# Two decoder layers on one core: a chunk's outputs issued with the next chunk's work, a merge in halves, and a longer pause in front of the scores

## The chip, the core and the metric

The kernel runs on one core of one Trainium2 chip. The core has five engines with an instruction queue each: TensorE (PE, matrix products, with its weight loads shown apart as PEld), VectorE (DVE), ScalarE (ACT), GpSimd (POOL) and SyncE (SP, which here only issues DMAs). They run on their own and wait for each other through semaphores. The metric is the time of one execution on the device in microseconds (us), lower is better: the median of three runs before is 1919.49 us (1916.85 to 1920.4). In rows of the trace, L117 and L133 are lines of two helpers that issue every matmul and every VectorE or ScalarE operation, so an operation is known by its tiles, written out<-in.

## What is computed

Two layers of a decoder, 256 tokens, width 2048, all in float32. The first joins an RG-LRU and an mLSTM group; the change doesn't touch it. The second is RWKV-7 time mixing with 64 heads of 64: an input projection gives r, k, v and a gate z, low-rank paths give the decay w and the rate a, and each head carries a 64x64 state S from token to token:

```python
def step(S, inp):
    r_t, w_t, k_t, v_t, kk_t, a_t = inp
    sa = jnp.einsum('bhvk,bhk->bhv', S, -kk_t)
    S = (S * w_t[:, :, None, :] + sa[..., None] * (kk_t * a_t)[:, :, None, :]
         + v_t[..., None] * k_t[:, :, None, :])
    return S, jnp.einsum('bhvk,bhk->bhv', S, r_t)
...
kk = (k * k_k).astype(jnp.float32).reshape(B, S, H, d)
kk = kk / jnp.maximum(jnp.sqrt(jnp.sum(kk * kk, axis=-1, keepdims=True)), 1e-12)
...
y = rwkv7_scan(rh, wh, kh, vh, kk, ah)
y = head_norm(y.reshape(B, S, RWKV_WIDTH), H, RWKV_GN_EPS, gn_g, gn_b)
bonus = jnp.sum(rh * kh * r_k.astype(jnp.float32), axis=-1, keepdims=True) * vh
y = (y + bonus.reshape(B, S, RWKV_WIDTH)).astype(h.dtype)
return (y * jax.nn.silu(z)) @ w_out
```

The kernel takes the 256 tokens in four chunks of 64. Inside a chunk the dependence of the tokens on each other becomes a triangular system of 64x64 for each head, which is inverted once; from chunk to chunk the state is carried.

## The kernel before

**Projections.** The second layer works in eight groups g of eight heads (four tiles f of 128 features, two heads hd in each). A group has four projections in the order k, r, z, v (`in_proj`, line 242), each of eight pieces. A piece loads 512 KB of weights, splits them in a rounded part whi (ScalarE, CAST) and the rest wlo (VectorE) in `split_w` (line 202), and multiplies: hh·whi and hl·whi in turn, then hh·wlo, 24 matmuls of 128x256 a piece (`in_mms`, line 221) into banks called `gb`. hh and hl are the two parts of the normed input. whi and wlo have three buffers each. The splits are emitted at a higher priority than other work, so that the scheduler puts them ahead of it on ScalarE and VectorE.

**Weaving.** The rest of a group is written as Python generators in five lanes of `Weave` (line 58). After every four projection matmuls `tick(0.44)` moves a planner's clock on, and generators whose time has come are advanced; what they issue stands at that place in PE's order, which `InOrder` makes fixed. A `yield w` asks for w planner's microseconds before the next piece; after a piece with matmuls other generators are held back for 0.4. So a larger number in a yield moves the matmuls behind it later among the projection's, and whatever is later in the same lane with it. Lane 0 has `blocks` and `inverse`, lane 1 `scores`, `values` and `recur`, lane 2 the first half of `norm`, lane 3 `decay` and `keys`, lane 4 `outs`. Small matmuls write banks called `mb`, of which there are four.

**The pieces.** `keys` (line 851) works on the shifted k (kt, from `shifted`, line 806: a ScalarE copy and a VectorE operation for each of four tiles): squares sq on ScalarE, eight matmuls `cs,sq` for the norms, Gn from them, the product kP, and then eight times xx and zz (ScalarE, three buffers in common) and BK = xx·zz (VectorE); AR holds kk times the decay. `blocks` (line 891) multiplies BK by AR, 32 matmuls of 64x64 in four quarters, and VectorE makes Aab from them. `inverse` (line 950) eliminates on VectorE in blocks of 32 and merges them: 32 matmuls `ZT,Aab`, two copies to ZT on ScalarE, 32 matmuls `TT,ZT`, two copies to TT. `scores` (line 915) writes r times the decay into the other half of AR (four VectorE operations, line 919), pauses (`yield 2`, line 921), and makes At and the transposed BKt from AR and BK, tile by tile. `recur` (line 1043) then goes through the chunks c: W from UV and At; Ws, a copy; U from Ws and TT; UV, U times Gn on VectorE; S from UV and BKt; the new state Sn on VectorE, copied into the next chunk's UV by ScalarE; the outputs from UV and At; and, from c = 1 on, the outputs of the state before, from Rc and that state. W, U, S and each kind of output are eight matmuls. After c = 1 `norm` of the first 128 tokens is added in lane 2; that of the rest is done in `outs`.

**Groups overlap.** The recurrence of group g runs while the k projection and the r projection of group g+1 are on PE, so it meets `keys` and `blocks` of group g+1, on PE as on VectorE and ScalarE.

Of the kernel before, what the change touches and what calls it, by code (L numbers as in the profile page):

```python
# [7 lines left out]
F32 = mybir.dt.float32  # L8
# [3 lines left out]
ADD, SUB, MUL, MAX, MIN = ALU.add, ALU.subtract, ALU.mult, ALU.max, ALU.min  # L12

P = 128
# [130 lines left out]
def two_layers(ctx, tc, x, gpost, cst, selc, v0, v1, w_in0, w_out0, w_in1, w_out1, lruw, qkvw,  # L145
               wif, gbias, lora1, lora2, out):
    nc = tc.nc
    act, dve, pool, pe = nc.scalar, nc.vector, nc.gpsimd, nc.tensor
    PS = bass.MemoryType.PSUM
    wv_ = Weave(tc, 5)  # L150
    pe = wv_.pe = InOrder(tc, pe)
    dve, act = Behind(tc, dve), Behind(tc, act)
# [13 lines left out]
    def mbank():  # L166
        return pm.tile([P, 512], F32, name="mb", tag="mb")
# [252 lines left out]
    with ExitStack() as l0:  # L420
# [4 lines left out]
        def t4(name):  # L425
            return tp.tile([P, 4, T], F32, name=name, tag="t4")
# [315 lines left out]
    with ExitStack() as l1:  # L742
        c1 = l1.enter_context(tc.tile_pool(name="c1", bufs=1))
        g1 = l1.enter_context(tc.tile_pool(name="g1", bufs=1))
# [170 lines left out]
        def scores(g, st):  # L915
            rt, AR, BK, Pe = st["r"], st["AR"], st["BK"], st["Pe"]
            yield 0.36
            for f in range(4):
                dve.tensor_tensor(AR[:, f, :, 64:128], c4(rt[:, f, :]), Pe[:, 4 * f:4 * f + 4, 1:65], MUL)
                yield 0.5  # L920
            yield 2
            Rc = gt("Rc", "Rc", (4, 4, 64))
            act.copy(Rc, AR[:, :, :, 64:128])

            At = gt("At", "At", (4, 2, 4, 128))
            BKt = gt("BKt", "BKt", (4, 4, 128))
            rm4 = rmask.unsqueeze(1).broadcast_to([P, 4, 128])
            for f in range(4):
                ab = [mbank(), mbank()]
                for c in range(4):  # L930
                    for hd in range(2):
                        hr = slice(64 * hd, 64 * hd + 64)
                        pe.matmul(ab[hd][:, 128 * c:128 * c + 128], lhsT=BK[hr, f, c, :], rhs=AR[hr, f, c, :],
                                  start=(c == 0), stop=True, skip_group_check=True)
                b = mbank()
                for c in range(4):
                    pe.transpose(out=b[:, c * P:(c + 1) * P], in_=BK[:, f, c, :], identity=ident)
                yield 0.42
                for hd in range(2):
                    v = ab[hd].rearrange("p (c j) -> p c j", c=4)  # L940
                    dve.tensor_tensor(At[:, f, hd, :, :], v, rm4, MUL)
                    yield 1.12
                act.copy(BKt[:, f, :, :], b.rearrange("p (c j) -> p c j", c=4))
            for hd in range(2):
                hr = slice(64 * hd, 64 * hd + 64)
                act.copy(At[hr, :, hd, :, 0:64], AR[hr, :, :, 0:64])
                yield 0.3
            st.update(At=At, BKt=BKt, Rc=Rc)

        def inverse(g, st):  # L950
            Aab = st["Aab"]

            Ab, Tb, ZT = (t4(n, (32, 32), parts=64) for n in ("Ab", "Tb", "ZT"))
# [17 lines left out]
            TT = gt("TT", "TT", (32, 64))  # L971
# [8 lines left out]
            Amm = Aab.rearrange("p f h c i -> p (f h c) i")  # L980
            halves = [slice(16 * hf, 16 * hf + 16) for hf in range(2)]
            zb = [mbank(), mbank()]
            for m in range(32):
                pe.matmul(zb[m // 16][32:64, 32 * (m % 16):32 * (m % 16) + 32], lhsT=Amm[0:32, m, 32:64], rhs=ZT[0:32, m, :],
                          start=(m % 16 == 0), stop=True, skip_group_check=True)
            for hf, ms in enumerate(halves):
                act.copy(ZT[32:64, ms, :], zb[hf][32:64, :].rearrange("p (m c) -> p m c", m=16))
            yield 2.4
            tb = [mbank(), mbank()]
            for m in range(32):  # L990
                pe.matmul(tb[m // 16][0:32, 32 * (m % 16):32 * (m % 16) + 32], lhsT=ZT[32:64, m, :], rhs=TT[32:64, m, 32:64],
                          start=(m % 16 == 0), stop=True, skip_group_check=True)
            for hf, ms in enumerate(halves):
                act.copy(TT[0:32, ms, 32:64], tb[hf][0:32, :].rearrange("p (m c) -> p m c", m=16))
            yield 1.28

            TTv = TT.rearrange("p (f h c) i -> p f h c i", f=4, h=2)
            act.copy(TTv[64:128, :, 0, :, :].rearrange("p f c i -> p f (c i)"), TTv[0:64, :, 1, :, :].rearrange("p f c i -> p f (c i)"))
# [44 lines left out]
        def recur(g, st):  # L1043
            yield from until(st["inv"])
            At, BKt, UV, Rc, Gn, PC, TTv = (st[n] for n in ("At", "BKt", "UV", "Rc", "Gn", "PC", "T"))

            vt = st["v"]
            Yn = gt("Yn", "Yn", (2, 4, 2, 64))
            Yb = None
            St = None  # L1050
            for c in range(4):
                wb = mbank()
                for f in range(4):
                    for hd in range(2):
# [18 lines left out]
                Sp = St  # L1073
                if c < 3:
                    sb = mbank()
                    for f in range(4):
                        for hd in range(2):
                            hr = slice(64 * hd, 64 * hd + 64)
                            pe.matmul(sb[hr, f * 64:(f + 1) * 64], lhsT=BKt[:, f, c, hr], rhs=UV[:, c, f, hd, :],
                                      start=(f == 0), stop=True, skip_group_check=True)  # L1080
                    Sn = g1.tile([P, 4, 64], F32, name="Sn", tag="Sn", bufs=2)
                    sv = sb[:, 0:256].rearrange("p (f v) -> p f v", f=4)
                    pcb = PC[:, :, c:c + 1].broadcast_to([P, 4, 64])
                    if c:
                        dve.tensor_tensor(Sn, St, sv, ADD)
                        dve.tensor_tensor(Sn, Sn, pcb, MUL)
                    else:
                        dve.tensor_tensor(Sn, sv, pcb, MUL)
                    for hd in range(2):
                        hr = slice(64 * hd, 64 * hd + 64)  # L1090
                        act.copy(UV[hr, c + 1, :, hd, :], Sn[hr])
                    St = Sn
                    yield 2.4

                if c % 2 == 0:
                    Yb = [mbank(), mbank()]
                cr = [slice(64 * ((c + hd) % 2), 64 * ((c + hd) % 2) + 64) for hd in range(2)]
                for f in range(4):
                    for hd in range(2):
                        pe.matmul(Yb[hd][cr[hd], f * 64:(f + 1) * 64], lhsT=At[:, f, hd, c, 64:128],  # L1100
                                  rhs=UV[:, c, f, hd, :], start=(f == 0),
                                  stop=(c == 0), skip_group_check=True)
                yield 0.2
                if c:
                    for f in range(4):
                        for hd in range(2):
                            hr = slice(64 * hd, 64 * hd + 64)
                            pe.matmul(Yb[hd][cr[hd], f * 64:(f + 1) * 64], lhsT=Rc[hr, f, c, :],
                                      rhs=Sp[hr, f, :], start=False, stop=True, skip_group_check=True)
# [199 lines left out]
```

## Time and profile before

| | us |
|---|---|
| runs before, median (lowest, highest) | 1919.49 (1916.85, 1920.4) |
| the profiled execution | 1918.59 |
| its span in the profile | 1916.8 |
| PE busy | 1889.9 |
| DVE busy | 1395.0 |
| ACT busy | 1045.3 |
| mean granted clock of PE | 0.994 of full speed |

The span is the profiled execution from its first to its last instruction. Busy times are those in which at least one instruction of an engine was running; matmuls overlap in PE's pipeline, so starts tell more of their pace than durations. A row of the waits reads: engine and output waited on, the operation that released it, us in total, how often, the longest. A row of the timeline reads: start, duration, engine, operation with its tiles and shapes, how many were put together, and in brackets the idle time just before and what ended it. A row of the windows has its stretch, its length, the busy time and count of PE, PEld, DVE, ACT and POOL, then the granted clock, the share of DMA and GB/s. A row of the groups has busy time and mean ns behind the first bar, and the engine's idle time just before and what ended it behind the second.

### The profile page before, as it was taken

To read this page: it belongs to the slowest core of one execution; us is meant where nothing else is said; L and a number is where in the kernel's file an instruction comes from. 1 tells how busy PE (TensorE), PEld (TensorE's weight loads), DVE (VectorE), ACT (ScalarE), POOL (GpSimd) and SP (SyncE) were. 2 spreads that over 40 slices of the span, in tenths; PEclk is the share of its full clock that TensorE was granted. 3 is DMA by queue.
4 is the path that set the end of the run, shared out by engine and by line. 5 is a ranking of instruction groups with operands and counts; after the bars stand their busy time and mean duration, and the time that the engine had idled before them with its cause. 6 is when DMAs were issued, how large, how long until landed. Compare 5 with 4: busy or idle time off the path is not lost.

```text
span 1916.8 us, 39532 instructions
## 1 busy us (share of the span) xinstructions
PE 1889.9 (99%) x16507; PEld 1752.9 (91%) x16507; DVE 1395.0 (73%) x2302; ACT 1045.3 (55%) x1609; POOL 58.4 (3%) x84
## 2 busy tenths in 40 slices
PE   9999999999999999999999999999999999999998
PEld 8999999999888899989999999999999999997886
DVE  5667777767555579879689689597696896895544
ACT  6445666645444546555565555655655655555442
POOL 0000000000000000000000000000000000000000
PEclk9999999999999999999999999999999999999999
DMA  7333445445655444433343334344343343355664
GB/s 255 138 132 111 176 165 171 154 171 199 212 203 204 161 148 143 155 106 137 133 140 133 133 130 157 109 147 143 114 154 133 130 144 133 122 184 191 224 202 156
DMA packets 86947, 299.63 MB, mean 156 GB/s; under 512 B 9576, under 2 KB 12392, under 8 KB 86768
## 3 DMA queue, kind: packets, MB, share of 16 engines
q1 hardware_dynamic: 86768, 297.11, 45.0%
q8 instruction: 129, 2.11, 0.4%
q14 instruction: 50, 0.41, 0.1%
HBM read 289.20 MB, written 7.86 MB: 155 GB/s over the span
## 4 chain that ended last, share of the span: by engine, by line
PE 92%; DVE 5%; ACT 1%; issue 1%; DMA 1%; POOL 0%; SPq 0%; DVEq 0%; POOLq 0%; ACTq 0%
PE gb L117 74%; PE mb L117 17%; DVE wlo L133 2%; PE mb L120 1%; ACT whi L133 1%; DVE wb L133 1%; DMA raw<-in_w_in_dram 0%; DVE rt L133 0%; DVE Tb L133 0%; DMA xq<-in_x_dram 0%; DVE Yn L133 0%; DVE tf L133 0%; DVE Ab L133 0%; ACT ZT L133 0%; DVE At L133 0%
## 5 line engine op out<-in xcount | busy, mean ns | idle before, releaser
L133 DVE TENSOR_TENSOR wlo<-raw,whi 128x1024 fp32r<-128x1024 f32 x509 | 619.9, 1219 | 343.6 <-ACT whi L133 310.3
L133 ACT CAST whi<-raw 128x1024 fp32r<-128x1024 f32 x509 | 532.2, 1048 | 555.3 <-PE gb L117 500.8
L117 PE MATMUL gb<-hh,whi 128*128 128x256 f32 x3120 | 793.5, 290 | 2.9 <-ACT whi L133 2.9
L117 PE MATMUL gb<-hl,whi 128*128 128x256 f32 x3120 | 773.7, 284 | 0.6 <-DVE hl L133 0.6
L117 PEld LDWEIGHTS gb<-hh,whi 128*128 128x128 f32 x3120 | 598.5, 192 | 13.8 <-ACT whi L133 3.7
L117 PEld LDWEIGHTS gb<-hl,whi 128*128 128x128 f32 x3120 | 599.5, 192 | 2.0 <-DVE hl L133 1.2
L117 PE MATMUL gb<-hh,wlo 128*128 128x256 f32 x3120 | 453.5, 286 | 0.0
L117 PEld LDWEIGHTS gb<-hh,wlo 128*128 128x128 f32 x3120 | 405.0, 191 | 4.2 <-issue 0.7
L117 PE MATMUL gb<-whi,yl 128*128 128x512 f32 x500 | 136.9, 392 | 0.5 <-DVE yl L133 0.5
L117 PE MATMUL gb<-whi,yh 128*128 128x512 f32 x500 | 136.5, 392 | 0.0
L117 PE MATMUL gb<-wlo,yh 128*128 128x512 f32 x500 | 135.7, 390 | 0.0
L117 PEld LDWEIGHTS gb<-whi,yl 128*128 128x128 f32 x500 | 93.2, 188 | 20.4 <-DVE yl L133 0.9
L117 PEld LDWEIGHTS gb<-wlo,yh 128*128 128x128 f32 x500 | 93.5, 188 | 19.7
L117 PEld LDWEIGHTS gb<-whi,yh 128*128 128x128 f32 x500 | 92.9, 188 | 19.3
L133 DVE TENSOR_TENSOR Tb<-Tb,tf 64x31 f32<-64x31 f32 (+15 forms) x248 | 82.7, 333 | 6.3
L133 DVE TENSOR_TENSOR tf<-Ab,Tb 64x31 f32<-64x31 f32 (+15 forms) x248 | 82.1, 331 | 4.4
L117 PE MATMUL mb<-AR,BK 64*128 64x128 f32 (+1 forms) x1024 | 57.4, 253 | 7.0 <-DVE AR L133 6.0
L117 PEld LDWEIGHTS mb<-AR,BK 64*128 64x128 f32 (+1 forms) x1024 | 49.7, 161 | 13.2 <-PE gb L117 7.1
L133 DVE TENSOR_TENSOR UV<-mb,Gn 64x256 f32<-64x256 f32 x64 | 27.0, 421 | 34.5 <-PE mb L117 33.3
L133 ACT ACTIVATE zz<-kP,dv 128x256 f32<-128x256 f32 x64 | 32.3, 505 | 22.9 <-DVE kP L133 12.4
L117 PEld LDWEIGHTS mb<-UV,At 128*64 128x64 f32 (+1 forms) x1024 | 35.0, 137 | 10.3 <-issue 2.2
L117 PE MATMUL mb<-UV,At 128*64 128x64 f32 (+1 forms) x1024 | 43.8, 228 | 0.0
(259 smaller groups left out, 1844.4 us busy)
## 6 DMA issues: line engine op xcount, KB each, us to landing
raw<-in_w_in_dram SPq DMA_DIRECT2D x384, 512.0 KB, 3.3
raw<-in_w_out_dram SPq DMA_DIRECT2D x128, 512.0 KB, 4.3
y1d<-zt SPq DMA_DIRECT2D x7, 512.0 KB, 3.5
yraw<-y1d SPq DMA_DIRECT2D x7, 512.0 KB, 3.9
l<-in_lora_dram SPq DMA_DIRECT2D x8, 384.0 KB, 4.4
xq<-in_x_dram SPq DMA_DIRECT2D x8, 256.0 KB, 4.6
lw<-in_lruw_dram SPq DMA_DIRECT2D x4, 512.0 KB, 4.8
xr<-in_x_dram SPq DMA_DIRECT2D x8, 256.0 KB, 7.1
```

The costliest lines, as they stand in the source:

```text
L117: return self._chain(self.eng.matmul(*a, **k))
L120: return self._chain(self.eng.transpose(**k))
L133: r = op(*a, **k)
```

## The change

Three things change in the second layer.

In `scores`, the pause between AR and the matmuls that read it is 3.4 instead of 2.

In `inverse`, each of the two runs of 32 matmuls becomes two of 16, each followed at once by its copy; a pause stands behind each half (1.6 for ZT, 1.5 for TT) instead of behind the whole (2.4 and 1.28).

In `recur`, the outputs from UV of chunk c-1 are issued just ahead of W of chunk c, the outputs of the state just behind U, and only the last chunk's outputs from UV stand alone. `norm` of the first 128 tokens is added behind W of chunk 2, since the outputs of chunk 1 are complete there. The pauses behind W, U and the new state are 1.6, 2.2 and 4.0 instead of 1.4, 1.8 and 2.4 (with 0.2 and 0.25 behind the outputs).

```diff
@@ scores
-            yield 2
+            yield 3.4
@@ inverse
-            for m in range(32):
-                pe.matmul(zb[m // 16][32:64, 32 * (m % 16):32 * (m % 16) + 32], lhsT=Amm[0:32, m, 32:64], rhs=ZT[0:32, m, :],
-                          start=(m % 16 == 0), stop=True, skip_group_check=True)
             for hf, ms in enumerate(halves):
+                for m in range(16 * hf, 16 * hf + 16):
+                    pe.matmul(zb[hf][32:64, 32 * (m % 16):32 * (m % 16) + 32], lhsT=Amm[0:32, m, 32:64], rhs=ZT[0:32, m, :],
+                              start=(m % 16 == 0), stop=True, skip_group_check=True)
                 act.copy(ZT[32:64, ms, :], zb[hf][32:64, :].rearrange("p (m c) -> p m c", m=16))
-            yield 2.4
+                yield 1.6
...
-            yield 1.28
+                yield 1.5
@@ recur
+            def outputs(c, Yb):
+                for f in range(4):
+                    for hd in range(2):
+                        o = slice(64 * ((c + hd) % 2), 64 * ((c + hd) % 2) + 64)
+                        pe.matmul(Yb[hd][o, f * 64:(f + 1) * 64], lhsT=At[:, f, hd, c, 64:128],
+                                  rhs=UV[:, c, f, hd, :], start=(c == 0 and f == 0), stop=True, skip_group_check=True)
+
             for c in range(4):
+
+                if c:
+                    outputs(c - 1, Yb)
                 wb = mbank()
...
-                yield 1.4
+                if c == 2:
+                    nm = wv_.add(norm(0, Yb, Yn, Yn[:, 1]), 2)
+                yield 1.6
                 ub = mbank()
...
+                if c % 2 == 0:
+                    Yb = [mbank(), mbank()]
+                if c:
+                    for f in range(4):
+                        for hd in range(2):
+                            hr = slice(64 * hd, 64 * hd + 64)
+                            o = slice(64 * ((c + hd) % 2), 64 * ((c + hd) % 2) + 64)
+                            pe.matmul(Yb[hd][o, f * 64:(f + 1) * 64], lhsT=Rc[hr, f, c, :],
+                                      rhs=St[hr, f, :], start=(f == 0), stop=False, skip_group_check=True)
                 for hd in range(2):
                     hr = slice(64 * hd, 64 * hd + 64)
                     dve.tensor_tensor(UV[hr, c, :, hd, :], ub[hr, 0:256].rearrange("p (f v) -> p f v", f=4),
                                       Gn[hr, :, c:c + 1].broadcast_to([64, 4, 64]), MUL)
-                yield 1.8
...
+                yield 2.2
+                if c == 3:
+                    outputs(c, Yb)
+                    yield 0.4
+                    break
...
+                yield 4.0
-                if c % 2 == 0:
-                    Yb = [mbank(), mbank()]
...
-                yield 0.2
...
-                    yield 0.25
-                if c == 1:
-                    nm = wv_.add(norm(0, Yb, Yn, Yn[:, 1]), 2)
```

**How it moves instructions on PE.** The recurrence of group 1 beside the keys of group 2, before. `UV,At` are outputs from UV (or W, which has the same form), `Sn,Rc` outputs of the state, `cs,sq` the norms; each stands alone between projection matmuls.

```order
L117 MATMUL mb<-Sn,Rc 64x64 x8
L117 MATMUL gb<-hh,whi 128x256
L117 MATMUL gb<-hl,whi 128x256
L117 MATMUL gb<-hh,whi 128x256
L117 MATMUL gb<-hl,whi 128x256
L117 MATMUL mb<-UV,At 64x64 x8
L117 MATMUL gb<-hh,wlo 128x256 x8
L117 MATMUL mb<-cs,sq 128x2 x8
```

The same place now, from the outputs with W (`UV,At` x16) on; `Ws,TT` is U.

```order
L117 MATMUL gb<-hh,wlo 128x256 x8
L117 MATMUL mb<-UV,At 64x64 x16
...
L117 MATMUL mb<-Ws,TT 64x64 x8
L117 MATMUL mb<-Sn,Rc 64x64 x8
L117 MATMUL gb<-hh,whi 128x256
L117 MATMUL gb<-hl,whi 128x256
```

Between the norms and `blocks` of a later group stood nine runs of eight before (U, S, outputs and W by turns), and now two of sixteen and one of eight; the 80 projection matmuls between them are as many as before.

**On VectorE, from the end of the k projection to the norms of group 2**, before. `kt` is the shifted k, `AR` its product with the decay, `wlo` a weight split, `Sn` the state of group 1, `Gn` the first operation behind the norms.

```order
L133 TENSOR_TENSOR wlo<-raw,whi 128x1024
L133 SCALAR_TENSOR_TENSOR kt<-gb,vec_81,kt 128x255 x2
L133 SCALAR_TENSOR_TENSOR AR<-kt,vec_81,Pe 128x4x64
L133 SCALAR_TENSOR_TENSOR kt<-gb,vec_81,kt 128x255
L133 SCALAR_TENSOR_TENSOR AR<-kt,vec_81,Pe 128x4x64
L133 SCALAR_TENSOR_TENSOR kt<-gb,vec_81,kt 128x255
L133 SCALAR_TENSOR_TENSOR AR<-kt,vec_81,Pe 128x4x64 x2
L133 TENSOR_TENSOR wlo<-raw,whi 128x1024
L133 TENSOR_SCALAR Gn<-mb 64x8 x4
```

And now:

```order
L133 SCALAR_TENSOR_TENSOR kt<-gb,vec_81,kt 128x255
L133 TENSOR_TENSOR wlo<-raw,whi 128x1024
L133 SCALAR_TENSOR_TENSOR kt<-gb,vec_81,kt 128x255 x2
L133 SCALAR_TENSOR_TENSOR AR<-kt,vec_81,Pe 128x4x64 x3
L133 TENSOR_TENSOR wlo<-raw,whi 128x1024
L133 SCALAR_TENSOR_TENSOR kt<-gb,vec_81,kt 128x255
L133 TENSOR_TENSOR Sn<-Sn,mb 128x256
L133 SCALAR_TENSOR_TENSOR AR<-kt,vec_81,Pe 128x4x64
L133 TENSOR_TENSOR Sn<-Sn,PC 128x256
L133 TENSOR_SCALAR Gn<-mb 64x8 x4
```

Two weight splits instead of one stand among the four kt, one of them ahead of the last kt; the state of group 1 has moved from ahead of kt to between it and Gn.

**On VectorE, the last BK of group 2 and Aab behind them**, before (`vr` is of the norm of group 1's outputs):

```order
L133 TENSOR_TENSOR UV<-mb,Gn 64x4x64 x2
L133 TENSOR_TENSOR BK<-xx,zz 128x4x64
L133 TENSOR_TENSOR wlo<-raw,whi 128x1024
L133 TENSOR_TENSOR BK<-xx,zz 128x4x64 x2
L133 TENSOR_TENSOR Aab<-mb,Gn 64x2x256 x2
L133 TENSOR_REDUCE vr<-At 128x8
```

And now:

```order
L133 TENSOR_TENSOR BK<-xx,zz 128x4x64
L133 TENSOR_TENSOR Sn<-Sn,PC 128x256
L133 TENSOR_TENSOR wlo<-raw,whi 128x1024
L133 TENSOR_TENSOR BK<-xx,zz 128x4x64
L133 TENSOR_TENSOR Aab<-mb,Gn 64x2x256
L133 TENSOR_TENSOR BK<-xx,zz 128x4x64
```

The first product behind `blocks` (Aab) stood behind the last BK and now stands between the last ones: `blocks` has moved forward against the key work.

More of the change, by code (lines that the diff above doesn't have):

```diff
@@ L982, in inverse @@
             zb = [mbank(), mbank()]
-            for m in range(32):
-                pe.matmul(zb[m // 16][32:64, 32 * (m % 16):32 * (m % 16) + 32], lhsT=Amm[0:32, m, 32:64], rhs=ZT[0:32, m, :],
-                          start=(m % 16 == 0), stop=True, skip_group_check=True)
             for hf, ms in enumerate(halves):
+                for m in range(16 * hf, 16 * hf + 16):
+                    pe.matmul(zb[hf][32:64, 32 * (m % 16):32 * (m % 16) + 32], lhsT=Amm[0:32, m, 32:64], rhs=ZT[0:32, m, :],
+                              start=(m % 16 == 0), stop=True, skip_group_check=True)
                 act.copy(ZT[32:64, ms, :], zb[hf][32:64, :].rearrange("p (m c) -> p m c", m=16))
-            yield 2.4
+                yield 1.6
             tb = [mbank(), mbank()]
-            for m in range(32):
-                pe.matmul(tb[m // 16][0:32, 32 * (m % 16):32 * (m % 16) + 32], lhsT=ZT[32:64, m, :], rhs=TT[32:64, m, 32:64],
-                          start=(m % 16 == 0), stop=True, skip_group_check=True)
             for hf, ms in enumerate(halves):
+                for m in range(16 * hf, 16 * hf + 16):
+                    pe.matmul(tb[hf][0:32, 32 * (m % 16):32 * (m % 16) + 32], lhsT=ZT[32:64, m, :], rhs=TT[32:64, m, 32:64],
+                              start=(m % 16 == 0), stop=True, skip_group_check=True)
                 act.copy(TT[0:32, ms, 32:64], tb[hf][0:32, :].rearrange("p (m c) -> p m c", m=16))
-            yield 1.28
+                yield 1.5
             TTv = TT.rearrange("p (f h c) i -> p f h c i", f=4, h=2)
@@ L1071, in recur @@
                                       Gn[hr, :, c:c + 1].broadcast_to([64, 4, 64]), MUL)
-                yield 1.8
[L1073 to L1088, printed above, removed]
+                yield 2.2
@@ L1089, in recur @@
+                if c == 3:
+                    outputs(c, Yb)
+                    yield 0.4
+                    break
+                sb = mbank()
+                for f in range(4):
                     for hd in range(2):
                         hr = slice(64 * hd, 64 * hd + 64)
-                        act.copy(UV[hr, c + 1, :, hd, :], Sn[hr])
-                    St = Sn
-                    yield 2.4
-                if c % 2 == 0:
-                    Yb = [mbank(), mbank()]
-                cr = [slice(64 * ((c + hd) % 2), 64 * ((c + hd) % 2) + 64) for hd in range(2)]
@@ L1098, in recur @@
[L1098 to L1102, printed above, removed]
-                yield 0.2
-                if c:
[L1105 to L1109, printed above, removed]
-                    yield 0.25
@@ L1111, in recur @@
-                if c == 1:
-                    nm = wv_.add(norm(0, Yb, Yn, Yn[:, 1]), 2)
+                        pe.matmul(sb[hr, f * 64:(f + 1) * 64], lhsT=BKt[:, f, c, hr], rhs=UV[:, c, f, hd, :],
+                                  start=(f == 0), stop=True, skip_group_check=True)
+                Sn = g1.tile([P, 4, 64], F32, name="Sn", tag="Sn", bufs=2)
+                sv = sb[:, 0:256].rearrange("p (f v) -> p f v", f=4)
+                pcb = PC[:, :, c:c + 1].broadcast_to([P, 4, 64])
@@ L1113, in recur @@
+                if c:
+                    dve.tensor_tensor(Sn, St, sv, ADD)
+                    dve.tensor_tensor(Sn, Sn, pcb, MUL)
+                else:
+                    dve.tensor_tensor(Sn, sv, pcb, MUL)
+                for hd in range(2):
+                    hr = slice(64 * hd, 64 * hd + 64)
+                    act.copy(UV[hr, c + 1, :, hd, :], Sn[hr])
+                St = Sn
+                yield 4.0
             st.update(nm=nm, Yb=Yb, Yn=Yn, At=At)
```

## Prediction

> **What bounds the kernel now.** I read the page's busy times and its chain first, then the waits of TensorE, then its timeline around the places that the change touches, then ScalarE and VectorE there, and last the granted clock by windows.
>
> ```profile
> PE 1889.9 (99%) x16507; PEld 1752.9 (91%) x16507; DVE 1395.0 (73%) x2302; ACT 1045.3 (55%) x1609; POOL 58.4 (3%) x84
> PE 92%; DVE 5%; ACT 1%; issue 1%; DMA 1%; POOL 0%; SPq 0%; DVEq 0%; POOLq 0%; ACTq 0%
> ...
> PE mb L117 <- DVE AR L133: 6.0, 6, 1.0
> PE mb L117 <- ACT ZT L133: 1.7, 6, 0.3
> PE mb L117 <- ACT sq L133: 1.0, 2, 0.8
> PE mb L117 <- DVE BK L133: 0.8, 1, 0.8
> ```
>
> TensorE (PE) is busy 99% of the span and makes 92% of the chain that ended last. It works through one fixed order, so whatever shortens that order, or a pause in it, shortens the kernel one for one; VectorE (DVE, 73%) and ScalarE (ACT, 55%) count only where PE waits for them. The four waits are of the changed stretch, in us in total, times, longest: two are aimed at (AR in `scores`, ZT in the merge); the other two, sq at the norms and BK at `blocks`, are rare today. The sum is made against the profiled execution, 1918.59 us with a span of 1916.8; the median of the three runs is 1919.49.
>
> **Step 1, fewer and longer runs of small matmuls.** PE's rows alternate between projection matmuls (out `gb`) and runs of small ones (out `mb`). The trace records each matmul twice, so x16 is eight.
>
> ```profile
> 1075.22 0.28 PE L117 MATMUL gb<-hl,whi 128*128 128x256 f32 x1
> 1075.43 0.68 PE L117 MATMUL mb<-Ws,TT 64*64 64x64 f32 x16
> 1076.04 0.39 PE L117 MATMUL gb<-hh,whi 128*128 128x256 f32 x1
> 1076.26 0.28 PE L117 MATMUL gb<-hl,whi 128*128 128x256 f32 x1
> ...
> 844.44 0.28 PE L117 MATMUL gb<-hl,whi 128*128 128x256 f32 x1
> 844.65 2.08 PE L117 MATMUL mb<-AR,BK 64*64 64x64 f32 x64
> 846.66 0.74 PE L117 MATMUL gb<-hh,wlo 128*128 128x256 f32 x4
> 847.33 0.68 PE L117 MATMUL mb<-Ws,TT 64*64 64x64 f32 x16
> ```
>
> Starts matter, since durations overlap. Undisturbed projection matmuls start 0.12 us apart. From 1075.22 to 1076.26 lie two of them and one run of 16 records: 1.04 - 0.24 = 0.80 us for the run. The run of 64 lies between 844.44 and the run at 847.33, which enters 0.21 after the last of four wlo matmuls (as 1075.43 follows 1075.22): 847.12 - 844.44 - 4 x 0.12 = 2.20 us. So 48 records more cost 1.40, 0.029 each, and each run has about 0.80 - 16 x 0.029 = 0.33 us of its own, for going in and out. By the rows of the order, each of the eight groups has six runs fewer in the recurrence (outputs from UV joined to W three times, the state's outputs to U three times) and two more in the merge (two halves of Z and of T). 48 - 16 = 32 runs fewer at 0.33: **-10.6 us**. Bounds: nothing, if the price belongs to the records and not to the run, and -15.8 if the new halves cost no entry. I take the middle, since the same rows price both.
>
> **Step 2, the waits aimed at.**
>
> ```profile
> 1001.02 0.28 PE L117 MATMUL gb<-hl,whi 128*128 128x256 f32 x1
> 1002.31 1.16 PE L117 MATMUL mb<-AR,BK 64*128 64x128 f32 x16 [1.01 <-DVE AR L133]
> ```
>
> The first run of `scores` starts 1.29 us after the matmul ahead of it where a run without a wait starts 0.21 after: 1.08 lost, six times (the AR row above). The pause is 1.4 longer in the planner's time, so the last AR is done when PE arrives: 6 x -1.08 = **-6.5**. The merge's second run no longer follows the copies of both halves but, after two gaps of 16 projection matmuls (1.9 us each), that of its own half: the 1.7 us of the ZT row go, **-1.7**. The two rows are their own bounds, since a wait can give back no more than it has; what is late next stands in steps 3 and 4.
>
> Dependencies inside the recurrence get new distances: Ws is copied under 12 to 16 projection matmuls (1.4 to 1.9 us), UV is multiplied under 20 (2.4 us). I cost these at nothing; with the cover gone each would be a fraction of a microsecond, 24 times.
>
> **Step 3, the norms (`cs,sq`).** The order shows that in groups 2 to 7 VectorE now has a weight split (wlo) ahead of the last shifted k, as only group 1 had before. What that does can be read in group 1, beside group 2 without it:
>
> ```profile
> 823.02 0.95 PE L117 MATMUL mb<-cs,sq 128*128 128x2 f32 x8
> 825.55 0.61 PE L117 MATMUL mb<-cs,sq 128*128 128x2 f32 x4 [0.82 <-ACT sq L133]
> 964.36 1.84 PE L117 MATMUL mb<-cs,sq 128*128 128x2 f32 x16
> ...
> 822.25 1.05 ACT L133 CAST whi<-raw 128x1024 fp32r<-128x1024 f32 x1 [0.47 <-PE gb L117]
> 823.33 1.23 DVE L133 TENSOR_TENSOR wlo<-raw,whi 128x1024 fp32r<-128x1024 f32 x1 [0.52 <-ACT whi L133]
> 824.48 0.48 DVE L133 SCALAR_TENSOR_TENSOR kt<-gb,vec,kt 128x255 f32<-128x255 f32 x1
> 824.99 0.51 ACT L133 ACTIVATE sq<-kt,vec 128x256 f32<-128x256 f32 x1 [0.92 <-DVE kt L133]
> ```
>
> The split's cast waits for PE to release a buffer, wlo for the cast, kt for wlo, the square for kt, and PE for the square. The norms last 826.16 - 823.02 = 3.14 us against 1.84: 1.30 lost. My walk along the new rows, each started when its engine and its inputs are free, gives 1.2 in groups 2 to 7, so I take 1.3, with 0 (the cast a little earlier) and 2.5 (a whole wlo more) as ends. Group 1 loses its split there and gets about 0.9 back. 6 x 1.3 - 0.9 = **+6.9** (-0.9 to +14).
>
> **Step 4, `blocks` (`AR,BK`).**
>
> ```profile
> 982.61 2.30 PE L117 MATMUL mb<-AR,BK 64*64 64x64 f32 x64
> 983.75 0.42 DVE L133 TENSOR_TENSOR BK<-xx,zz 128x256 f32<-128x256 f32 x1 [1.90 <-ACT zz L133]
> 959.05:984.18 25.13, 25.09 (x348) 22.59 (x346) 18.19 (x36) 20.05 (x42) 2.74 (x2) 1.00 0.33 116
> L133 ACT CAST whi<-raw 128x1024 fp32r<-128x1024 f32 x509 | 532.2, 1048 | 555.3 <-PE gb L117 500.8 <-issue 29.1 <-ACT Yn L133 5.6
> L133 ACT ACTIVATE xx<-fa,dv 128x256 f32<-128x256 f32 x64 | 37.8, 591 | 0.0
> L133 ACT ACTIVATE zz<-kP,dv 128x256 f32<-128x256 f32 x64 | 32.3, 505 | 22.9 <-DVE kP L133 12.4 <-DVE BK L133 10.3
> L133 DVE TENSOR_TENSOR wlo<-raw,whi 128x1024 fp32r<-128x1024 f32 x509 | 619.9, 1219 | 343.6 <-ACT whi L133 310.3 <-ACT xx L133 11.5 <-ACT thr L133 4.7
> L133 DVE TENSOR_TENSOR BK<-xx,zz 128x256 f32<-128x256 f32 x64 | 27.1, 423 | 18.4 <-ACT zz L133 17.9
> L133 DVE TENSOR_TENSOR kP<-kt,th 128x1024 f32<-128x1024 f32 x8 | 9.8, 1225 | 0.2
> ```
>
> In group 2 the last of the eight BK ends at 984.17, 19.8 us after the norms began (964.36), and the run of `blocks` already lasts 2.30 instead of 2.08: its last quarter waited 0.22. ScalarE was busy 20.05 of 25.13 us there (second-last of the pairs of numbers in the window's row). Between norms and `blocks` PE had 80 projection matmuls (9.6 us), the norms and nine runs of 16 (7.2). It keeps the 80, but the runs become two of 32 (0.33 + 32 x 0.029 = 1.27 each) and one of 16: 3.3 us. So the same work meets PE some 3.5 us sooner: `blocks` is due 18.25 - 3.5 = 14.8 us after the norms are due, with step 3's pause 16.0, and its last quarter 1.55 later, at 17.55.
>
> The key work in those rows: the norms' pause and kP end after about 5.0 us; then eight times xx (0.59), zz (0.51) and BK (0.42), with three buffers for xx and zz, and four weight splits (1.05 on ScalarE, then 1.22 on VectorE) put ahead of them. Walking them through as above, BK 1 ends at 7.7, BK 4 at 13.4, BK 7 at 18.3 and BK 8 at 19.3. The last quarter then waits 19.3 - 17.55 = 1.8 us, where 0.2 was lost before: 6 x 1.6 = **+9.6**. The ends: scaling ScalarE's 20.05 us by its 36 operations against 42 and letting it never idle gives 17.2, no pause (-1.3 in all); the chain of group 1 of before, 21.4 us from its norms to its last BK, gives 3.9 (+22). I take my walk, which lies near the 19.8 of group 2.
>
> **Step 5, the granted clock.**
>
> ```profile
> 929.50:932.90 3.40, 3.22 (x73) 3.18 (x74) 3.28 (x7) 3.26 (x7) 0.00 (x0) 1.00 0.57 207
> 932.90:936.30 3.40, 3.40 (x19) 3.40 (x18) 0.00 (x0) 1.53 (x3) 0.00 (x0) 0.50 0.46 155
> 1462.00:1465.40 3.40, 3.40 (x18) 3.40 (x17) 0.00 (x1) 1.45 (x3) 0.00 (x0) 0.50 0.48 154
> 823.67:827.08 3.41, 2.44 (x29) 2.13 (x30) 3.24 (x10) 0.91 (x3) 0.00 (x0) 1.00 0.42 150
> 827.08:830.49 3.41, 3.41 (x24) 3.29 (x21) 2.04 (x4) 0.62 (x2) 0.00 (x0) 0.50 0.02 6
> 1005.30:1008.70 3.40, 3.40 (x37) 3.15 (x36) 3.37 (x8) 2.58 (x4) 0.13 (x1) 1.00 0.21 80
> ```
>
> The third number from the end is the granted clock. In the middle of the kernel five windows of 3.41 us ran at half speed: one behind the norms' pause of group 1 (from 827.08), four behind the merge's second run (the first and the last are shown), out of eight merges. Each is worth half its length, 1.7 us. What comes ahead is a window with few projection matmuls. Halved merges have 1.9 us of projection between the halves, so I let the four go, and that of group 1: -8.5. The twelve new pauses (six at the norms, six at `blocks`) leave windows as thin; by the five hits in nine such places seven of them would be followed by half speed: 7 x 1.7 = +11.9. Together **+3.4**, with -8.5 (no new one) and +11.9 (all twelve, 20.4) as ends.
>
> The Trainium skill ("TensorE: Matmul & The Clock Gate", Part 1: The HAM clock gate) gives half speed only after at least one idle window of about 3.4 us. The window ahead of 932.90 had PE busy 3.22 of 3.40 us and half speed followed all the same, so here the trace does not bear the rule out in that form. By the rule, no pause named here would change the clock; that is the first rival.
>
> **Sum**: -10.6 - 6.5 - 1.7 + 6.9 + 9.6 + 3.4 = +1.1 us, so 1919.7 on the profiled execution and 1920.6 on the median. I forecast **1920**, its own range 1914 to 1926 from a third of a group's pause either way.
>
> **Rivals.** (a) *The new pauses leave the clock alone*: 11.9 less, 1908. For it: none of the six AR pauses of 1.0 us was followed by half speed (the window from 1005.30, behind the one at 1002.31, ran at 1.00). Against: that of group 1, which is of the very kind. (b) *The key work keeps up*: ScalarE has six operations fewer to do, `blocks` doesn't wait, and about four half-speed windows fall away too: 1920 - 10.8 - 6.8 = 1902. Against it: VectorE's BK sits behind weight splits, which go first. (c) *Slower*: one mechanism, the key chain at `blocks`. From a chain of 20 us on, 0.2 longer than in group 2 of before, the kernel is measurably slower; at 21.4, as in group 1, the pause is 3.9 and the time 1920 + 6 x 2.1 = 1933. For it: the norms' pause, now in every group, is what group 1 had. (d) *The merging saves nothing*, because the price lies at a change of shape between W and outputs: 10.6 more, 1931. Against it: outputs from UV and W have the same form, as have the state's outputs and U.
>
> **How the numbers follow.** Forecast 0.46, (a) 0.18, (b) 0.13, (c) 0.18, (d) 0.05. A measurement of this kernel can tell about 0.2%, 3.8 us. Faster than 1915.6: (a), (b) and a quarter of the forecast, 0.43. Slower than 1923.3: (c), (d) and a fifth of it, 0.32. The rest, 0.25, is within. The range from 1902 to 1931 leaves out half of (b), most of (c) and the tails.
>
> **What would show it.** Step 1: runs of x32 (outputs with W, U with the state's outputs) that take about 1.27 us between projection matmuls. Step 2: no AR or ZT row among PE's waits. Step 3: an sq row of about six times 1.2. Step 4: BK, or the zz ahead of it, waited for about 1.8 us in six groups. Step 5: half-speed windows behind those two places, none behind the merge. The forecast is wrong if the sq and BK rows stay as small as now (then 1902 or lower), or if BK's is twice as long.

## The result and the profile after

The changed kernel takes 1930.36 us (median; 1928.89 to 1932.42) where the kernel before took 1918.25 beside it: ratio 1.0063, 95% interval 1.005 to 1.0075. It is slower by some 12 us. The profiled execution took 1931.68 us with a span of 1929.9, 13.1 more than before.

The page's busy times and chain, and then TensorE's waits (us in total, times, longest), of the changed kernel:

```profile
PE 1892.1 (98%) x16506; PEld 1756.8 (91%) x16507; DVE 1398.2 (72%) x2302; ACT 1046.7 (54%) x1609; POOL 71.1 (4%) x84
PE 76%; DVE 16%; ACT 3%; POOL 2%; issue 2%; DMA 1%; SPq 0%; POOLq 0%; DVEq 0%; ACTq 0%
...
PE mb L117 <- DVE BK L133: 8.5, 17, 0.9
PE mb L117 <- ACT sq L133: 6.0, 13, 0.8
PE mb L117 <- DVE At L133: 5.5, 13, 0.8
...
PE mb L117 <- ACT UV L133: 2.0, 1, 2.0
```

Busy times hardly differ; the chain does: 16% of it now lies on VectorE where 5% did. Of the waits, AR and ZT are gone, sq and BK have come as forecast, and two are new, which the prediction had not counted on: At in the scores, and one wait of 2.0 us for UV in the recurrence of group 1.

Where the time went can be summed from TensorE's timeline: for each run of small matmuls the time between the projection matmul ahead of it and the second one behind it, less 2 x 0.12 us (2 x 0.22 for the last group's runs, which stand among the larger matmuls of the output projection), over the second layer. Half-speed windows are those of 3.41 us in the second layer, outside the kernel's last microseconds; some of the time that they cost lies inside the rows. These sums are used for the experiments too:

| us in the profiled execution | before | after |
|---|---|---|
| runs of the recurrence (144, then 96) | 119.9 | 102.1 |
| runs of the merge (16, then 32) | 39.6 | 42.2 |
| scores (32) | 62.1 | 68.4 |
| norms (8) | 15.6 | 24.2 |
| blocks (8) | 20.2 | 32.7 |
| half-speed windows | 5 | 9 |

The recurrence gave 17.8 us. Scores, norms and blocks took 6.3 + 8.6 + 12.5 = 27.4, part of it as half speed, and the merge 2.6: +12.2 in the rows, where the span grew by 13.1. The rows behind the table, from TensorE's timeline of the changed kernel: first one run of outputs and W, then norms and blocks of one group, then the second tile of the scores:

```profile
1239.86 1.15 PE L117 MATMUL mb<-UV,At 128*64 128x64 f32 x32
1240.94 0.39 PE L117 MATMUL gb<-hh,whi 128*128 128x256 f32 x1
...
1233.80 0.95 PE L117 MATMUL mb<-cs,sq 128*128 128x2 f32 x8
1234.92 0.61 PE L117 MATMUL mb<-cs,sq 128*128 128x2 f32 x4 [0.17 <-ACT sq L133]
1236.34 0.61 PE L117 MATMUL mb<-cs,sq 128*128 128x2 f32 x4 [0.82 <-ACT sq L133]
...
1251.32 0.67 PE L117 MATMUL mb<-AR,BK 64*64 64x64 f32 x14 [0.16 <-DVE BK L133]
1252.32 0.32 PE L117 MATMUL mb<-AR,BK 64*64 64x64 f32 x2 [0.33 <-DVE BK L133]
1253.50 0.67 PE L117 MATMUL mb<-AR,BK 64*64 64x64 f32 x14 [0.86 <-DVE BK L133]
...
1280.14 0.48 PE L117 MATMUL mb<-AR,BK 64*128 64x128 f32 x2
1281.40 1.16 PE L117 MATMUL mb<-AR,BK 64*128 64x128 f32 x14 [0.78 <-DVE At L133]
```

The merged run takes 1.27 us by the measure above, as worked out. The norms' rows repeat group 1 of before to a hundredth (0.16 and 0.82 there). The run of blocks stops three times for a BK. The second tile of the scores stops after its first matmul: a tile takes three of the four `mb` banks, so its second bank must be freed by At of the first tile, and that is late. Ahead of the last four of the eight BK, VectorE also waits for GpSimd, in the norm of the group before:

```profile
1248.43 0.69 DVE L133 TENSOR_TENSOR Yn<-Yn,vr 128x512 f32<-128x512 f32 x1 [0.74 <-POOL vr L1151]
```

In the kernel before, this Yn stood between the second BK and the third (1236.56), without a wait; the change adds that norm later, and the prediction's sum has no term for it. No run here moves the norm alone, so what it costs at blocks stays open.

The windows behind the pauses (clock: third number from the end):

```profile
962.20:965.60 3.40, 2.56 (x22) 2.39 (x21) 3.21 (x7) 2.34 (x5) 0.00 (x0) 1.00 0.45 159
969.00:972.40 3.40, 3.40 (x22) 3.17 (x22) 0.21 (x1) 1.95 (x3) 0.00 (x0) 0.50 0.00 0
982.70:986.10 3.40, 2.12 (x54) 1.72 (x50) 2.98 (x6) 2.29 (x6) 0.00 (x0) 1.00 0.55 178
986.10:989.50 3.40, 3.40 (x26) 3.06 (x21) 2.75 (x3) 0.79 (x1) 0.00 (x0) 0.50 0.26 94
```

Half speed follows the norms (from 965.6 on, for two windows; the second is shown) and blocks, behind windows in which PE was busy 2.56 and 2.12 of 3.40 us. Of the twelve pauses at norms and blocks of groups 2 to 7, five were followed by half speed, in seven windows (groups 2, 3 and 7), and seven were not. Busy time alone doesn't tell them apart: the window 1119.20:1122.61, behind the blocks of group 3, had PE busy 2.32 us and was followed by full speed. What does, no run here shows. The other two windows lie behind the norms of group 1 (from 825.7), whose wait had shrunk to 0.15 us, and behind the UV wait (from 866.6).

### The profile page after: what moved, and what is told of

Read it like the earlier page. It is cut to its first block, busy times and chain, and to the rows that moved or that the text cites. A ratio compares the mean times of both kernels' runs of the same rounds, so it can differ in the third digit from the quotient of the medians.

```text
span 1929.9 us, 39539 instructions
## 1 busy us (share of the span) xinstructions
PE 1892.1 (98%) x16506; PEld 1756.8 (91%) x16507; DVE 1398.2 (72%) x2302; ACT 1046.7 (54%) x1609; POOL 71.1 (4%) x84
## 4 chain that ended last, share of the span: by engine, by line
PE 76%; DVE 16%; ACT 3%; POOL 2%; issue 2%; DMA 1%; SPq 0%; POOLq 0%; DVEq 0%; ACTq 0%
PE gb L117 64%; PE mb L117 12%; DVE wlo L133 4%; POOL vr L1151 2%; DVE Tb L133 2%; DVE tf L133 2%; DVE At L133 1%; ACT whi L133 1%; DVE Ab L133 1%; DVE Yn L133 1%; DVE Aab L133 1%; DVE vr L133 1%; DVE rt L133 1%; DVE wb L133 1%; DVE BK L133 1%
## 5 line engine op out<-in xcount | busy, mean ns | idle before, releaser
L117 PEld LDWEIGHTS gb<-hh,whi 128*128 128x128 f32 x3120 | 600.7, 193 | 12.2 <-ACT whi L133 3.7
L117 PEld LDWEIGHTS gb<-wlo,yh 128*128 128x128 f32 x500 | 93.4, 188 | 19.7
L117 PEld LDWEIGHTS gb<-whi,yh 128*128 128x128 f32 x500 | 93.4, 188 | 19.6
L117 PE MATMUL mb<-AR,BK 64*128 64x128 f32 (+1 forms) x1024 | 69.1, 257 | 14.2 <-DVE BK L133 8.5
L117 PEld LDWEIGHTS mb<-AR,BK 64*128 64x128 f32 (+1 forms) x1024 | 56.1, 161 | 25.3 <-DVE BK L133 11.3
L1151 POOL TENSOR_TENSOR vr<-vr,mhalf 128x8 f32<-128x8 f32 x16 | 40.3, 2517 | 515.5 <-DVE vr L133 515.5
L133 ACT COPY BKt<-mb 128x512 f32<-128x512 f32 x32 | 19.1, 598 | 72.3 <-PE mb L120 72.3
```

The lines of the kernel that those rows point to most:

```text
L117: return self._chain(self.eng.matmul(*a, **k))
L133: r = op(*a, **k)
L1151: pool.tensor_tensor(vr, vr, mhalf[:, 0:8], ALU.pow)
```

## The experiments

**First, the parts alone, and the scores.** The At row asked for a cause. Theory L put it down to the new recurrence, which ends later, so that the outputs of the group before meet the scores on VectorE; rival P put it down to the pause itself. Each part of the change was run alone, and the whole with a still longer pause:

```diff
# pause_alone: scores of the kernel before
-            yield 2
+            yield 3.4
# halves_alone: the change's part in inverse; recur_alone: its part in recur
# after_pause6: scores of the changed kernel
-            yield 3.4
+            yield 6.0
```

> The kernel before with the longer pause in front of the scores (3.4 for 2) and nothing else. Theory L (late outputs): the wait of the scores moved to their second tile in the changed kernel because the new recurrence ends later and the previous group's outputs then meet the scores on VectorE. Without the new recurrence that doesn't happen, so the AR wait (6.0 us) goes, no At row appears among TensorE's waits, and the time is 6 us lower, ratio 0.997. Rival P (the pause itself): the later scores meet other work of VectorE, an At row of about 5 us takes the place of the AR row, and the ratio is 1.000.

> The kernel before with the merge in halves and nothing else. Theory: sixteen runs more cost 16 x 0.3 = +4.9 us, the ZT waits give back 1.7 to 2.3, and the four half-speed windows behind the merge's second run (1.7 us each) go with them: together about -4 us, ratio 0.998. Rival (the clock doesn't care): the four windows stay or turn up elsewhere, and the ratio is 1.0015.

> The kernel before with the new recurrence and nothing else. Theory L: the runs of the recurrence cost about 18 us less, the norms 8 us more and blocks 12 us more, and the scores wait longer than before (for AR or for a bank that At frees), 6 us or more in all: 1927 to 1932 us, ratio 1.005 to 1.007. Rival P: the scores lose no more than before, since their pause is the old one, and the ratio is 1.001 or lower.

> The changed kernel with a pause of 6.0 in front of the scores for 3.4: on TensorE only the scores move, by 20 projection matmuls (2.4 us) or so. Theory L: the previous group's outputs are then done on VectorE when the scores' first products come; the At row (5.5 us) falls below 1.5 and the time is 1930 - 7 = 1923. Rival P: a longer pause makes the At row no smaller, and the time stays within 2 us of 1930 or rises.

| | ratio to before (95%) | recurrence | merge | scores | norms | blocks | half-speed windows |
|---|---|---|---|---|---|---|---|
| pause_alone | 1.0031 (1.002 to 1.0042) | 120.3 | 39.8 | 65.4 | 16.2 | 20.2 | 4 |
| halves_alone | 0.9971 (0.9961 to 0.998) | 119.5 | 42.2 | 62.3 | 14.7 | 20.2 | 1 |
| recur_alone | 1.0049 (1.0034 to 1.0064) | 100.2 | 39.6 | 63.2 | 23.4 | 32.0 | 9 |
| after_pause6 | 1.0084 (1.0064 to 1.0103) | 100.5 | 42.2 | 72.0 | 23.4 | 32.2 | 6 |

Theory L fell. The pause alone, with the old recurrence, makes the kernel slower, and a longer one in the changed kernel left its At row at 5.5 and made the scores' runs longer (72.0). The recurrence alone came at the time that L gave (1927.13), but its scores grew by 1.1 us and not by 6, so the number was luck. TensorE's timeline of the pause alone, tiles 1 to 3 of the scores of one group, and VectorE's last AR and its At behind tile 1:

```profile
1135.90 1.16 PE L117 MATMUL mb<-AR,BK 64*128 64x128 f32 x16
1140.46 1.69 PE L117 MATMUL mb<-AR,BK 64*128 64x128 f32 x16
1145.55 1.77 PE L117 MATMUL mb<-AR,BK 64*128 64x128 f32 x16
...
1138.98 0.41 DVE L133 TENSOR_TENSOR AR<-rt,Pe 128x256 f32<-128x256 f32 x1
1140.26 0.67 DVE L133 TENSOR_TENSOR At<-mb,cs 128x512 f32<-128x512 f32 x1
1141.11 0.68 DVE L133 TENSOR_TENSOR At<-mb,cs 128x512 f32<-128x512 f32 x1
```

Tile 1 no longer waits (1.16), but tiles 2 and 3 stretch by 0.5 to 0.6 us each with no wait named; I take it that some of their matmuls keep running while others wait for a bank. At of tile 1 starts 3.2 us behind the end of its products (1137.06), with the last two AR, a weight split and elimination steps of the inverse in between, and ends at 1140.93; only then can the second bank of tile 2 be filled. Rival P had the place and not the size: it gave an At row of about 5 us (measured 0.3, the rest inside the runs) and no change in time; the time rose by 5.6 us where the profile shows 2.9 more span and 3.3 more in the scores; the rest isn't accounted for.

The halves behaved as expected: sixteen runs more, four half-speed windows fewer, 5 us faster. The recurrence alone gave its 19.7 us and lost more than that together: 7.8 at the norms, 11.8 at blocks and up to 6.8 to four more half-speed windows.

**Second, the order on VectorE.**

```diff
# recur_kt_first: recur_alone, and in shifted and keys
+                with tc.high_priority(offset=3000 if sec == 1 and g else 0):
                     activ(o[:, f, :], u, AF.Copy, scale=col(omu, i))
                     dve.scalar_tensor_tensor(o[:, f, 1:T], u[:, 0:T - 1], vs("mu", i), o[:, f, 1:T], MUL, ADD)
...
+                with tc.high_priority(offset=3000 if g else 0):
                     activ(sq[:, f, :], kt[:, f, :], AF.Square, scale=vs("kk", 4 * g + f))
# recur_kt_blk: that, and in blocks (halves_recur_kt_blk: 4.6, with the halves)
-            yield 3.5
+            yield 5.2
# pause_space: pause_alone, and behind each At
-                    yield 1.12
+                    yield 1.4
```

> The new recurrence alone (old merge, old pause), with the shifted k and its squares of groups 1 to 7 put ahead of the weight splits on ScalarE and VectorE; TensorE's order is that of the new recurrence alone. Theory K (order on VectorE): the norms' pause is the split ahead of the last shifted k, so the norms' runs fall from 23.5 us to about 15.7 and the time from 1927 to 1919, while the pause at blocks stays near 2.1 us a group. Rival (the chain only moves): what the norms no longer wait is waited at blocks, whose run grows by 1.2 us a group, and the time stays at 1927.

> As the run before it, and blocks asked for 1.7 later (5.2 for 3.5), which puts it behind 12 more projection matmuls and one more run of 32, some 2.7 us later on TensorE. Theory K: the pause at blocks is TensorE coming too early against a key chain of about 19 us, so the runs of blocks fall from 32 us to about 20.5 and the time by some 12 us more, to about 1907. Rival (the key work is simply late): the later blocks and what follows them wait elsewhere (the merge, the recurrence), and less than 4 us are gained.

> New recurrence and merge in halves with the old pause of the scores, k first as above, and blocks 1.1 later (12 projection matmuls, 1.4 us). Theory: the gains add: 18 us of the recurrence's runs, 5 us of the halves (with the half-speed windows that go), a pause of about 0.7 us left at blocks in six groups: 1918 - 18 - 5 + 4 + 1 = about 1900. Rival (VectorE is full): the scores' and the outputs' waits grow by as much as is gained at the keys, and the time is 1910 or more.

> The kernel before with the longer pause in front of the scores and 1.4 for 1.12 behind each of the two At operations of a tile, so that the tiles of the scores lie 28 projection matmuls apart and not 24. Theory V (banks): with the longer pause VectorE puts At behind more elimination steps, and tiles 2 to 4 wait for the banks that At frees; 0.5 us more between tiles covers it, so the scores' runs fall from 65.4 us to about 55.5 and the time from 1923 to 1912. Rival (VectorE fills any gap with elimination steps): the runs stay above 62 us and the time above 1918.

| | ratio to before (95%) | recurrence | merge | scores | norms | blocks | half-speed windows |
|---|---|---|---|---|---|---|---|
| recur_kt_first | 1.0006 (0.9997 to 1.0016) | 103.4 | 39.8 | 61.1 | 14.4 | 41.8 | 6 |
| recur_kt_blk | 0.9894 (0.9879 to 0.9909) | 101.5 | 37.6 | 64.3 | 14.4 | 21.1 | 0 |
| halves_recur_kt_blk | 0.9962 (0.9948 to 0.9977) | 101.4 | 42.6 | 65.6 | 14.4 | 28.7 | 2 |
| pause_space | 1.0078 (1.0061 to 1.0095) | 120.4 | 51.5 | 58.0 | 15.6 | 20.2 | 11 |

The norms' pause is the weight split ahead of k: with k first it is gone. But the 9 us came back at blocks (32.0 to 41.8, 2 us of it half speed), as the rival said. The time fell by 8 us all the same, which theory K had predicted for the wrong reason: the gain stands in three half-speed windows fewer (5 us) and 2 us of the scores. A group of the recurrence alone, from the first shift of k to blocks, and the same group with k first:

```profile
1223.81 1.50 ACT L133 ACTIVATE kt<-gb,dv 128x256 f32<-128x256 f32 x3 [0.49 <-PE gb L117]
1245.37 2.03 PE L117 MATMUL mb<-AR,BK 64*64 64x64 f32 x48
1248.43 0.43 DVE L133 TENSOR_TENSOR BK<-xx,zz 128x256 f32<-128x256 f32 x1
...
1219.44 1.50 ACT L133 ACTIVATE kt<-gb,dv 128x256 f32<-128x256 f32 x3 [0.49 <-PE gb L117]
1238.43 1.26 PE L117 MATMUL mb<-AR,BK 64*64 64x64 f32 x34
1241.13 0.68 PE L117 MATMUL mb<-AR,BK 64*64 64x64 f32 x14 [1.44 <-DVE BK L133]
1242.13 0.32 PE L117 MATMUL mb<-AR,BK 64*64 64x64 f32 x2 [0.33 <-DVE BK L133]
1243.31 1.11 PE L117 MATMUL mb<-AR,BK 64*64 64x64 f32 x14 [0.86 <-DVE BK L133]
...
1242.83 0.43 DVE L133 TENSOR_TENSOR BK<-xx,zz 128x256 f32<-128x256 f32 x1
```

From the first shift, the last BK ends at 25.1 us in the one and at 23.8 in the other, 1.2 sooner; but TensorE reaches blocks at 21.6 and at 19.0, 2.6 sooner, 1.3 of it for the norms and the rest because a half-speed window in between (from 1231.1) is gone. So it waits 1.3 longer. TensorE comes too early, and it was enough to let it come later. With blocks behind 12 more projection matmuls and one more merged run, only the last quarter still waits:

```profile
1216.45 1.87 PE L117 MATMUL mb<-cs,sq 128*128 128x2 f32 x16
1234.68 1.72 PE L117 MATMUL mb<-AR,BK 64*64 64x64 f32 x50
1236.65 0.68 PE L117 MATMUL mb<-AR,BK 64*64 64x64 f32 x14 [0.24 <-DVE BK L133]
```

The runs of blocks were 20.7 us shorter, and the time 21.6: 1897.57 us, 1.1% faster than before, where about 1907 was expected. No half-speed window was left of the six, which the expectation hadn't counted. This version beats both kernels. With the halves added and blocks only 12 projection matmuls later, blocks still take 1.6 us more than before in six groups (4.05 for 2.42), and the halves' runs cost 5 us with no half-speed windows left to remove. The time, 1910.93, is 11 us above the expectation and where the rival put it (1910 or more); but the scores grew by 3.5 us only, so the rival's reason isn't shown either.

In pause_space, more distance between the tiles did take most of the waits out of the scores (58.0), and the time rose by 9 us more, 20 above the expectation. TensorE's waits and timeline there:

```profile
PE mb L117 <- ACT ZT L133: 9.3, 6, 1.8
...
1330.53 0.66 PE L117 MATMUL mb<-TT,ZT 32*32 32x32 f32 x15 [1.79 <-ACT ZT L133]
```

The wait went to the next place that needs VectorE, the merge: ScalarE makes the ZT copies there behind an operation (`bh`) that waits for VectorE's `bi`, and `bi` ends 3.39 us behind the start of the merge's first run, where it ended 1.89 behind it before. That fits a VectorE without room, which a row of the kernel before would have shown, from the scores of a group to the middle of its elimination (VectorE's is the third pair of numbers):

```profile
1264.00:1290.00 26.00, 25.00 (x233) 23.94 (x232) 25.35 (x55) 12.37 (x15) 0.13 (x1) 1.00 0.42 144
```

25.35 of 26.00 us, where the page's mean is 73%.

**Third, room on VectorE.** Ten elimination steps (4 to 13) of each inverse are left out, for timing alone, on an unchanged order of TensorE; and the whole change is mended as the recurrence was.

```diff
# before_less, pause_less, after_less: in inverse
+                if not 4 <= j < 14:
                     dve.tensor_tensor(tm, Ab[:, j + 1:32, j:j + 1].broadcast_to([64, n, w]), Tb[:, j:j + 1, 0:w].broadcast_to([64, n, w]), MUL)
                     dve.tensor_tensor(Tb[:, j + 1:32, 0:w], Tb[:, j + 1:32, 0:w], tm, ADD)
# after_kt_blk: the changed kernel with k and its squares first, and in blocks
-            yield 3.5
+            yield 5.7
```

> The kernel before with ten of the 31 elimination steps of each inverse (4 to 13, some 7 us of VectorE in the stretch of the scores) left out; TensorE's order is unchanged. Theory V (VectorE is behind there): the AR row (6.0 us) falls below 1, the scores' runs from 62 us to about 54.5, and the time to about 1910. Rival (AR is late for ScalarE's or the projection's sake): the AR row stays above 4 us.

> The longer pause alone, with the same ten elimination steps left out. Theory V: its scores fall to the same 54.5 us (from 65.4), and the time is within 2 us of the run before it: with VectorE free the pause is worth nothing either way. Rival (the pause itself puts the scores beside other work): the scores stay above 60 us.

> The changed kernel with the same ten elimination steps left out. Theory V: the At row (5.5 us) goes below 1 and the scores' runs fall from 68.4 us to about 55; norms and blocks keep their pauses (24 and 33 us), and the time is about 1930 - 14 = 1916. Rival (banks are held by the other work in front of At): the scores stay above 62 us.

> The whole change (recurrence, halves, pause of 3.4) with the shifted k and its squares ahead of the weight splits and blocks asked for 2.2 later (5.7 for 3.5); nothing is left out. If the pauses at norms and blocks are what the new recurrence costs, they go (24 to 14.5 us and 33 to 22 us) and the half-speed windows with them, the scores keep their 66 to 68 us, and the time is about 1904. Rival (VectorE has no room for it): merge or scores grow by more than 6 us and the time is above 1912.

| | ratio to before (95%) | recurrence | merge | scores | norms | blocks | half-speed windows |
|---|---|---|---|---|---|---|---|
| before_less | 0.9995 (0.9985 to 1.0004) | 119.6 | 39.9 | 60.1 | 15.6 | 20.2 | 4 |
| pause_less | 0.9937 (0.9921 to 0.9954) | 119.6 | 39.7 | 54.0 | 15.6 | 20.2 | 1 |
| after_less | 0.9985 (0.9975 to 0.9995) | 100.5 | 42.3 | 55.9 | 23.1 | 32.6 | 8 |
| after_kt_blk | 1.0161 (1.0146 to 1.0177) | 126.9 | 42.6 | 68.7 | 22.0 | 17.7 | 14 |

With room on VectorE the scores of the changed kernel lose their waits (68.4 to 55.9) and the time falls to 1915.38, within a microsecond of what theory V said. VectorE's share in the stretch of the scores is lower by then, as the row of pause_less for the same place shows (21.69 of 26.00 us, for 25.35):

```profile
1258.00:1284.00 26.00, 26.00 (x243) 24.98 (x242) 21.69 (x40) 13.71 (x17) 0.13 (x1) 1.00 0.50 165
```

The pause then does what it was costed at: from before_less to pause_less the scores fall by 6.1 us and three half-speed windows go, 11.3 us in time. Two expectations of V failed. The pause was to be worth nothing with VectorE free, and was worth 11.3 us. And before_less keeps its AR wait in full (the row still reads 6.0, 6, 1.0). The timeline of before says why: TensorE waits for the first of the four AR (the second row ends the wait), and VectorE has only steps 0 to 3 ahead of it, which were all kept:

```profile
1000.59 0.48 DVE L133 SCALAR_TENSOR_TENSOR rt<-gb,vec,rt 128x255 f32<-128x255 f32 x1
1001.75 0.41 DVE L133 TENSOR_TENSOR AR<-rt,Pe 128x256 f32<-128x256 f32 x1
```

ScalarE's part of that r was done at 997.41; in the 3.2 us up to 1000.59 VectorE has work of the group before (Yn, zt), weight splits and early elimination steps. Which of them to move was not tried. Nor was At put first on VectorE with every step kept, which would part the order there from the amount of work.

The last run, 44 us above its expectation, shows that the remedy isn't general. Blocks no longer wait (17.7), neither merge nor scores grew as its rival had said, but the recurrence does, at a place where it had never waited:

```profile
1228.21 0.33 PE L117 MATMUL mb<-UV,BKt 128*64 128x64 f32 x2 [0.99 <-DVE UV L133]
1229.85 0.68 PE L117 MATMUL mb<-UV,BKt 128*64 128x64 f32 x14 [1.31 <-DVE UV L133]
1231.04 3.37 PE L117 MATMUL mb<-cs,sq 128*128 128x2 f32 x16
...
1226.95 0.88 DVE L133 SCALAR_TENSOR_TENSOR AR<-kt,vec,Pe 128x256 f32<-128x256 f32 x2
1227.74 0.41 DVE L133 TENSOR_TENSOR UV<-mb,Gn 64x256 f32<-64x256 f32 x1
1228.11 1.23 DVE L133 TENSOR_TENSOR wlo<-raw,whi 128x1024 fp32r<-128x1024 f32 x1
1229.37 0.43 DVE L133 TENSOR_TENSOR UV<-mb,Gn 64x256 f32<-64x256 f32 x1
```

There the recurrence meets the shifted k on VectorE, UV stands behind k and a weight split, S waits for UV, and the norms behind S run at half speed (3.37 us for 1.87). With blocks at 4.6 and the old pause (halves_recur_kt_blk) the recurrence takes 101.4, so the longer pause or the later blocks brought the two together; which of them was not tried.

## Why the forecast was 10 us low

The time, 1930.36, lies near the upper end of the range (1902 to 1931), but the likeliest case was 1920, its own range ended at 1926, and the kernel is clearly slower, to which the prediction gave 0.32. On the profiled execution the sum was +1.1 us and the span grew by 13.1.

- **Step 2, the failed one.** "so the last AR is done when PE arrives: 6 x -1.08 = -6.5". PE waits at tile 1 for the first AR, not the last; the first was done, and the wait of tile 1 went. The last was not: in pause_alone it starts at 1138.98, 3.1 us after tile 1. The scores' runs grew by 6.3 us: 12.8 off, as much as the whole miss of 12.0; the misses of the other steps nearly cancel. The step asked what ends PE's wait and not what VectorE does in the time won. It was full there (25.35 of 26.00 us), so the later scores only put At behind a weight split and more elimination steps, and PE waited one tile later for banks. Shown by pause_alone, and by the three runs with steps left out. "what is late next stands in steps 3 and 4" was wrong: it was in step 2 itself. The new distances inside the recurrence, put at nothing, cost one wait of 2.0 us (UV in group 1) and the half-speed window behind it.
- **Step 1** was right in mechanism, and 2.9 us low in size: 32 runs fewer at 0.33, with the ZT waits 12.3 us in all; measured 17.8 - 2.6 = 15.2. An extra half costs 0.31 (2 x 1.32 for 2.33). Merged runs of odd chunks cost less than worked out (below).
- **Step 3** was right in mechanism and size: 1.30 a group, and the run with k first took it away.
- **Step 4** was right in mechanism. Its "3.5 us sooner" doesn't follow from the numbers beside it (7.2 - 3.3 = 3.9), but blocks came where it put them: in the group shown 16.1 us after the norms (forecast 16.0). The run lasted 2.2 us longer than an undisturbed one where nothing ran at half speed, not 1.8. Forecast +9.6, measured +12.5 with the half speed in it. The chain took 19.6 us from the norms' start in the group shown (1233.80 to the last BK at 1253.44), where 19.3 was worked out. That what the norms don't lose is waited for at blocks had not been seen.
- **Step 5**: seven new half-speed windows forecast, nine found, and none left from behind the merge (halves_alone shows that the halves remove them). +6.8 us at 1.7 each instead of +3.4, part of it inside the rows of norms and blocks. That seven lie behind the pauses is luck in part: five pauses brought them and not seven, two of these two windows each. The window of group 1 was to go and stayed.
- **Rivals.** (b) did not happen, and (a) only in part: seven of the twelve pauses left the clock alone, and five of 1.3 and 2 us brought half speed, as in the window from 986.10, behind one with PE busy 2.12 of 3.40 us. The Trainium skill's rule of an idle window ahead ("TensorE: Matmul & The Clock Gate", Part 1: The HAM clock gate) isn't borne out by that row either. (c) had the right side and nearly the time, 1933, by the wrong part: blocks waited 2.2 us a group and not 3.9. (d) is excluded by the 1.27 us of a merged run, where two runs took 1.60.

## What to carry to other kernels

A wait that ends on a nearly full engine can move on instead of going when the waiting work comes later: read that engine's share in a window around the wait, not its mean, and follow what it does with the time that is won. When work on the leading engine is drawn together, everything fed by another engine meets it earlier; here 18 us of saved runs were lost to key work that had kept its pace, and came back once that work was put first and the run that needs it 2.7 us later. A part of a change is best timed alone: two of the three parts were slower, and the one with the largest gain inside it was the worst.

## What the runs showed of the hardware

U and the state's outputs, issued eight and eight, cost 1.27 us together in chunk 2 but 1.10 in chunks 1 and 3. In these the timeline shows their matmuls starting in between each other (changed kernel, chunk 1 of group 3):

```profile
1228.15 0.51 PE L117 MATMUL mb<-Ws,TT 64*64 64x64 f32 x10
1228.45 0.27 PE L117 MATMUL mb<-Sn,Rc 64*64 64x64 f32 x2
1228.49 0.28 PE L117 MATMUL mb<-Ws,TT 64*64 64x64 f32 x3
```

In odd chunks the outputs go to the other half of the output partitions than U of the same head, so the two kinds use different 64x64 quarters of the array; in chunk 2 they use the same. The Trainium skill ("TensorEngine Tiling (Array Packing)", Tiling Modes) has different tiles work in parallel; 0.17 us of 1.27 agree with that, though no run here changed the quarters alone.
